# The bias of the attention's exponentials, made on ScalarE column by column instead of on VectorE

## The chip, the cores and the metric

The kernel runs on one core of a Trainium2 chip. The metric is the device time of one execution in microseconds. A core has TensorE (matrix products and transposes, with weight loads beside them), VectorE, ScalarE, GpSimd and SyncE, each with its own in-order queue of instructions; they wait for each other by semaphores. In the profile they are PE, PEld, DVE, ACT, POOL and SP.

## The reference

One layer of a hybrid encoder trunk for 2048 tokens of width 1024. After an RMSNorm a common projection feeds three groups of heads: a state-space layer, differential attention, and a gated linear recurrence (HGRN2). Their outputs go through one output projection and are added to the stream; then follow a second RMSNorm, a gated MLP with a causal convolution, and a last RMSNorm. The part that matters here is the attention, with 6 heads, two softmax maps to a head, and a bias that falls with distance:

```python
def attend(args):
    q_blk, blk = args
    q_pos = blk * Q_BLOCK + jnp.arange(Q_BLOCK)
    sc = jnp.einsum('bqhcd,bkhcd->bhcqk', q_blk, k).astype(jnp.float32) * scale
    dist = jnp.abs(q_pos[:, None] - k_pos[None, :]).astype(jnp.float32)
    visible = (k_pos[None, :] // CHUNK) <= (q_pos[:, None] // CHUNK)
    bias = jnp.where(visible[None], -slopes[:, None, None] * dist[None], MASK_VALUE)
    p = jax.nn.softmax(sc + bias[None, :, None], axis=-1)
    w = p[:, :, 0] - lam * p[:, :, 1]
    return jnp.einsum('bhqk,bkhd->bqhd', w, v)
```

`c` is the map (0 or 1), `h` the head, and a block has 128 queries. The softmax subtracts each row's maximum, so every block needs one number per query and map before its exponentials can run.

## The kernel before

The tokens are cut into 16 blocks of 128 queries. `phase_attn` runs twice, first over the blocks 0 to 7 of all six heads, then, in its lean form with fewer buffers, over the blocks 8 to 15: 96 pairs of head and block. For one of them `scores` does the following. For each map it makes the scores in pieces of up to 512 keys on TensorE (L832, into one of three PSUM tiles `t_ps`). VectorE adds the distance bias to a piece, writes it to the score tile `t_sc` (one for each map) and carries the running maximum in `t_mx`, a tile of 128 x 2 x 4 with a column for each map and piece (L836, with a short instruction after it that writes the maximum). When both maps are done, VectorE makes the bias of the exponentials, `t_nm`, for both maps at once (L843): minus the slope times the last maximum, plus the constant column `t_lk` of each map, which holds scale factors that the second map is joined with. Then ScalarE takes the exponential of each map in place, with that bias as an operand of one number per partition, and sums it up (L848; a load of the function table stands ahead of it where another function's table is in use).

Behind it come, some steps later, `joined` (VectorE: a reciprocal in L860, a factor in L861, and in L867 the second map added to the first with that factor), `parts` (the weights split into two float16 halves, ScalarE's cast in L890 and GpSimd's subtraction in L891, and then transposed by DMAs on SyncE's queue in L898), `values` (the products with V on TensorE, L913) and `put` (ScalarE reads them out of PSUM, L875 and L877).

The attention is not alone. It is one of two streams that `weave` joins, each with costs that say how far it may run ahead of the other: while the attention runs, the other stream does the HGRN2 group (tiles `g_`), an early part of the output projection (`o_`) and then the MLP (`f_`), whose splitting of numbers into float16 halves goes through the helper `split` (ScalarE in L55, VectorE or GpSimd in L61, L63 and L59). L1863 is a helper of the MLP that adds or subtracts on VectorE or GpSimd. The order in which the instructions of one engine finally stand is not the order of the program text: the program is built with a planner that simulates the engines' times and places what is ready,

```python
    with tile.TileContext(nc, schedule_with_timeline_sim=True) as tc:
        tile_trunk_kernel(tc, *args)
```

and it sets the semaphores by what each instruction reads and writes.

Of the kernel before, what the change touches and what calls it, by code (L numbers as in the profile page):

```python
# [13 lines left out]
AF = mybir.ActivationFunctionType  # L14
ALU = mybir.AluOpType
# [17 lines left out]
SLOPES = [2.0 ** (-8.0 * (i + 1) / NH) for i in range(NH)]  # L33
# [720 lines left out]
def phase_attn(K, A, QKd, Vd, Yd, i0, i1, s_bufs, lean):  # L754
# [5 lines left out]
    tc, nc = K.tc, K.nc  # L760
    V = nc.vector
    NT = i1 - i0
    LM = 128 * i1
    base, nlam, lk, gc = A.base, A.nlam, A.lk, A.gc
    with ExitStack() as es:
# [50 lines left out]
        def scores(h, i, sc):  # L816


            H = heads[h]
            n_ = i - i0  # L820
            L = 128 * (i + 1)
            qt = kq[h, i // 4]
            mx = mp.tile([128, 2, 4], F32, tag="mx", name="t_mx")
            nm = mp.tile([128, 2], F32, tag="nm", name="t_nm")
            bs = base[:, S - L:S]
            nchunk = (L + 511) // 512
            sc += [sp.tile([128, LM], F32, tag="s", name="t_sc") for c in range(2)]
            for c in range(2):
                for j in range(nchunk):
                    k0, k1 = 512 * j, min(L, 512 * (j + 1))  # L830
                    ps = ps_s.tile([128, 512], F32, tag="s", name="t_ps")
                    nc.tensor.matmul(  # L832
                        out=ps[:, 0:k1 - k0], lhsT=qt[:, c, 128 * (i % 4):128 * (i % 4) + 128],
                        rhs=H.k[:, c, k0:k1], start=True, stop=True,
                    )
                    V.tensor_tensor_reduce(  # L836
                        out=sc[c][:, k0:k1], in0=ps[:, 0:k1 - k0], in1=bs[:, k0:k1], scale=1.0,
                        scalar=-3e38 if j == 0 else mx[:, c, j - 1:j],
                        op0=ALU.add, op1=ALU.max, accum_out=mx[:, c, j:j + 1],
                    )  # L840
                    if c == 0 or j < nchunk - 1:
                        yield 1
            V.scalar_tensor_tensor(  # L843
                out=nm, in0=mx[:, :, nchunk - 1], scalar=-SLOPES[h], in1=lk,
                op0=ALU.mult, op1=ALU.add,
            )
            for c in range(2):
                nc.scalar.activation(  # L848
                    out=sc[c][:, 0:L], in_=sc[c][:, 0:L], func=AF.Exp, scale=SLOPES[h],
                    bias=nm[:, c:c + 1], accum_out=H.la[:, c, n_:n_ + 1],  # L850
                )
            yield 1
# [127 lines left out]
        for h in range(NH):  # L980
            if lean and h > 0:
                load_k(h)
            if h + 1 < NH and not lean:
                load_k(h + 1)
            heads[h] = Head(h)
            for i in range(i0, i1):
                if i % 4 == 0:
                    kq.pop((h, i // 4 - 1), None)
                    load_q(h, i // 4 + 1)
                if i == i0 + 4 and h + 1 < NH:  # L990
                    for n in range(len(stages)):
                        while queues[n] and queues[n][0][2][0] < h:
                            step(n)
                    load_v(h + 1)
                while len(queues[0]) > s_bufs // 2 - 1:
                    step(0)
                t = (h, i, [])
                n = 2 * (i // 4 + 1)
                for _ in scores(*t):
                    slot += 1  # L1000
                    behind()
                    yield (2 * (i + 1) + 1) / n
                enter(0, t)
            yield 4
# [1130 lines left out]
```

## Time and profile before

| | |
|---|---|
| time, median of 3 runs | 2758.4 us (2749.91 to 2762.81) |
| the profiled execution's own time | 2750.61 us |
| its span, from the first instruction to the last | 2748.9 us |
| granted TensorE clock, mean | 0.928 |
| busy: TensorE, VectorE, ScalarE, GpSimd | 88%, 70%, 46%, 49% of the span |
| first and last bias instruction (L843) | 424.0 and 1914.1 us |

How to read the rows that follow. A row of a group names the line, the engine, the operation, what it writes and reads, its shapes, and how often it ran; behind the first bar stand its busy time in us and the mean of one in ns, behind the second the time in which the engine sat idle just before it, and what ended that. A row of the timeline has the start (us from the span's start), the length, and the instruction. A row of waits has who waited for whom, the total in us, how many times, and the longest. In a row of stretches, the busy time of each engine is followed by its number of instructions.

### The profile page before, as it was taken

To read this page: it belongs to the slowest core of one execution; us is meant where nothing else is said; L and a number is where in the kernel's file an instruction comes from. 1 tells how busy PE (TensorE), PEld (TensorE's weight loads), DVE (VectorE), ACT (ScalarE), POOL (GpSimd) and SP (SyncE) were. 2 spreads that over 40 slices of the span, in tenths; PEclk is the share of its full clock that TensorE was granted. 3 is DMA by queue.
4 is the path that set the end of the run, shared out by engine and by line. 5 is a ranking of instruction groups with operands and counts; after the bars stand their busy time and mean duration, and the time that the engine had idled before them with its cause. 6 is when DMAs were issued, how large, how long until landed. Compare 5 with 4: busy or idle time off the path is not lost. (4 is left out here: it accounts for less than half of the span.)

```text
span 2748.9 us, 42509 instructions
## 1 busy us (share of the span) xinstructions
PE 2429.6 (88%) x15438; PEld 1365.9 (50%) x15438; DVE 1924.5 (70%) x3497; ACT 1255.9 (46%) x2270; POOL 1357.3 (49%) x1149
## 2 busy tenths in 40 slices
PE   5998888988988899759998888599989999999998
PEld 4655547767766665334443334244435444444444
DVE  7567746888888785698678998966464655455565
ACT  6333344666656453465446566533144433333221
POOL 5788602444534442267656866615232444444280
PEclk8999999999988878869999999799999999999999
DMA  7675555565665446655555566598785655554733
GB/s 242 234 222 196 172 159 120 117 139 121 112 142 126 92 116 180 165 132 146 180 174 150 168 165 173 185 285 260 256 285 184 219 158 150 162 157 138 282 97 123
DMA packets 556738, 473.06 MB, mean 172 GB/s; under 512 B 277296, under 2 KB 433264, under 8 KB 555504
## 3 DMA queue, kind: packets, MB, share of 16 engines
q1 hardware_dynamic: 534352, 429.97, 55.1%
q10 hardware_dynamic: 22176, 40.38, 4.0%
q8 instruction: 121, 1.98, 0.3%
q14 instruction: 89, 0.73, 0.1%
HBM read 290.35 MB, written 125.83 MB: 151 GB/s over the span
## 5 line engine op out<-in xcount | busy, mean ns | idle before, releaser
L96 PE MATMUL f_pm<-f_q,f_w 128*128 128x512 f16 x3696 | 839.2, 387 | 34.5 <-DVE f_u L1863 10.4
L96 PEld LDWEIGHTS <-f_w 128*128 128x128 f16 x3696 | 363.6, 99 | 502.7 <-issue 77.0
L1786 PE MATMUL f_pd<-f_dw,f_da 128*128 128x512 f16 x1848 | 411.0, 384 | 8.4 <-DVE f_r L1764 7.0
L891 POOL TENSOR_TENSOR t_sc<-t_sc 128x1024 f16<-128x1024 f32 (+7 forms) x144 | 256.8, 1796 | 274.4 <-ACT t_sc L890 247.1
L1786 PEld LDWEIGHTS <-f_da 128*128 128x128 f16 x1848 | 182.0, 99 | 231.5 <-issue 21.5
L848 ACT ACTIVATE t_sc<-t_sc,t_nm 128x128 f32<-128x128 f32 (+7 forms) x192 | 228.9, 1194 | 81.6 <-DVE t_nm L843 81.0
L832 PE MATMUL t_ps<-t_k,t_q 96*128 96x512 f16 (+2 forms) x480 | 168.9, 386 | 100.6 <-DVE t_mx L836 93.3
L836 DVE CUSTOM_DVE_ANT_0 t_sc<-t_ps,t_base,t_mx 128x512 f32<-128x512 f32 (+3 forms) x288 | 185.2, 644 | 24.7 <-PE t_ps L832 15.5
L61 DVE TENSOR_TENSOR f_a<-f_t,f_a 128x512 f16<-128x512 f32 x132 | 155.6, 1200 | 53.4 <-ACT f_a L55 53.0
L867 DVE SCALAR_TENSOR_TENSOR t_sc<-t_sc,t_a 128x1024 f32<-128x1024 f32 (+7 forms) x144 | 180.5, 1279 | 1.3
L96 PE MATMUL g_pv<-g_w,g_h 128*128 128x256 f16 x1152 | 154.3, 292 | 18.7 <-ACT g_w L55 11.8
L913 PEld LDWEIGHTS <-t_wt 128*128 128x128 f16 x2448 | 108.2, 104 | 110.2 <-DMA t_wt<-t_sc 49.2
L1863 POOL TENSOR_TENSOR f_t<-f_t,f_t 128x512 f32<-128x512 f32 x66 | 100.9, 1543 | 121.2 <-ACT f_a L55 109.8
L96 PE MATMUL g_pq<-g_h,g_w 128*128 128x256 f16 x1152 | 149.7, 288 | 10.4 <-DVE g_sg L1160 5.4
L913 PE MATMUL t_po<-t_v,t_wt 128*128 128x64 f16 x2448 | 121.5, 202 | 38.3 <-DMA t_wt<-t_sc 33.0
L1863 POOL TENSOR_TENSOR f_k<-f_k,f_k 128x512 f32<-128x512 f32 x88 | 124.7, 1417 | 59.3 <-ACT f_k L1895 26.0
L1617 DVE SCALAR_TENSOR_TENSOR f_t<-f_u,f_cw,f_t 128x1024 f32<-128x1024 f32 x88 | 125.5, 1426 | 32.5 <-ACT f_t L1615 31.7
L890 ACT CAST t_sc<-t_sc 128x1024 f16<-128x1024 f32 (+7 forms) x144 | 111.7, 792 | 77.9 <-DVE t_sc L867 73.6
L836 DVE CUSTOM_DVE_ANT_0 t_sc<-t_ps,t_base 128x512 f32<-128x512 f32 (+2 forms) x192 | 121.0, 633 | 34.8 <-PE t_ps L832 21.4
L96 PEld LDWEIGHTS <-g_h 128*128 128x128 f16 x1152 | 118.0, 104 | 50.6 <-issue 22.5
L55 ACT ACTIVATE f_a<-f_t 128x512 f16<-128x512 f32 x154 | 94.8, 627 | 96.4 <-DVE f_a L61 32.1
L55 ACT ACTIVATE f_w<-f_sum 128x512 f16<-128x512 f32 x110 | 69.1, 628 | 150.0 <-DVE f_sum L139 65.1
(335 smaller groups left out, 4490.0 us busy)
## 6 DMA issues: line engine op xcount, KB each, us to landing
f_w<-Wd SPq DMA_DIRECT2D x231, 256.0 KB, 3.0
Wd<-f_w SPq DMA_DIRECT2D x154, 256.0 KB, 2.1
Ad<-f_a ACTq DMA_DIRECT2D x154, 256.0 KB, 2.6
f_da<-Ad SPq DMA_DIRECT2D x42, 768.0 KB, 5.1
g_h<-Hd SPq DMA_DIRECT2D x24, 1024.0 KB, 6.7
f_dst<-in_w_down_dram SPq DMA_DIRECT2D x48, 512.0 KB, 4.6
o_wst<-in_w_out_dram SPq DMA_DIRECT2D x24, 512.0 KB, 5.5
f_wst<-in_w_gate_dram SPq DMA_DIRECT2D x22, 512.0 KB, 5.5
```

What stands on the lines that cost most here:

```text
L55: nc.scalar.activation(out=hi, in_=src, func=AF.Copy, scale=scale)
L61: nc.vector.tensor_tensor(out=lo, in0=src, in1=hi, op=ALU.subtract)
L96: nc.tensor.matmul(out=out, lhsT=lhs(a, k), rhs=rhs(b, k), start=(n == 0), stop=(n == 3 * nk - 1))
L832: nc.tensor.matmul(out=ps[:, 0:k1 - k0], lhsT=qt[:, c, 128 * (i % 4):128 * (i % 4) + 128], rhs=H.k[:, c, k0:k1], start=True, stop=True,)
L836: V.tensor_tensor_reduce(out=sc[c][:, k0:k1], in0=ps[:, 0:k1 - k0], in1=bs[:, k0:k1], scale=1.0, scalar=-3e38 if j == 0 else mx[:, c, j - ...
L848: nc.scalar.activation(out=sc[c][:, 0:L], in_=sc[c][:, 0:L], func=AF.Exp, scale=SLOPES[h], bias=nm[:, c:c + 1], accum_out=H.la[:, c, n_:n_ ...
L867: V.scalar_tensor_tensor(out=sc[0][:, k0:k1], in0=sc[1][:, k0:k1], scalar=a[:, 1:2], in1=sc[0][:, k0:k1], op0=ALU.mult, op1=ALU.add,)
L891: nc.gpsimd.tensor_tensor(out=hl[:, LM + k0:LM + k1], in0=sc[0][:, k0:k1], in1=hl[:, k0:k1], op=ALU.subtract,)
L913: nc.tensor.matmul(out=po, lhsT=wt[:, w, b, :], rhs=vt[:, b, 64 * v:64 * v + 64], start=(b == 0 and w + v == 0), stop=(b == i and w == 1),)
L1617: V.scalar_tensor_tensor(out=t0, in0=u[:, c:n + c], scalar=cw[:, c, m:m + 1], in1=t0, op0=ALU.mult, op1=ALU.add,)
L1786: nc.tensor.matmul(out=ps[t], lhsT=a[:, q, x, tk], rhs=w[:, y, q, :], start=(first and q + x + y == 0), stop=(last and q == n - 1 and y == 1),
L1863: eng.tensor_tensor(out=o, in0=a, in1=b, op=op)
```

## The change

The one VectorE instruction that made both columns of `t_nm` goes. In its place ScalarE makes each column just ahead of the exponential that uses it, with the function Identity, the slope as scale and the column of `t_lk` as bias: two short instructions for each pair of head and block, 192 in all. In the new file they stand in L844 and the exponential stays in L848.

```diff
-            V.scalar_tensor_tensor(
-                out=nm, in0=mx[:, :, nchunk - 1], scalar=-SLOPES[h], in1=lk,
-                op0=ALU.mult, op1=ALU.add,
-            )
             for c in range(2):
+                nc.scalar.activation(
+                    out=nm[:, c:c + 1], in_=mx[:, c, nchunk - 1:nchunk], func=AF.Identity,
+                    scale=-SLOPES[h], bias=lk[:, c:c + 1],
+                )
                 nc.scalar.activation(
                     out=sc[c][:, 0:L], in_=sc[c][:, 0:L], func=AF.Exp, scale=SLOPES[h],
                     bias=nm[:, c:c + 1], accum_out=H.la[:, c, n_:n_ + 1],
```

## The prediction, made before the changed kernel ran

> **What bounds the kernel now.** I read the page first: the busy shares, then the chain.
>
> ```profile
> PE 2429.6 (88%) x15438; PEld 1365.9 (50%) x15438; DVE 1924.5 (70%) x3497; ACT 1255.9 (46%) x2270; POOL 1357.3 (49%) x1149
> PE 27%; DVE 4%; DMA 4%; issue 3%; POOL 2%; ACT 2%; SPq 0%; DVEq 0%; ACTq 0%; POOLq 0%
> ```
>
> TensorE is busy for 88% of the span, but that is an average over stages, and the followed chain reaches only the last part. The edited line runs in the attention, so I read the busy times by stretch next (us of each stretch: PE, PEld, DVE, ACT, POOL, then clock, DMA share, GB/s).
>
> ```profile
> 424.00:700.00 276.00, 245.68 (x2554) 199.12 (x2551) 224.77 (x647) 172.36 (x436) 120.12 (x112) 0.93 0.58 123
> 700.00:1000.00 300.00, 256.23 (x2632) 202.92 (x2632) 246.82 (x602) 166.90 (x321) 139.92 (x113) 0.87 0.54 119
> 1000.00:1300.00 300.00, 246.65 (x1548) 131.01 (x1549) 226.61 (x425) 152.04 (x269) 140.63 (x92) 0.82 0.60 154
> 1300.00:1600.00 300.00, 264.38 (x1425) 121.45 (x1423) 244.85 (x337) 152.05 (x255) 200.47 (x131) 0.96 0.56 166
> 1600.00:1790.00 190.00, 144.61 (x892) 68.01 (x891) 172.08 (x281) 118.03 (x183) 126.70 (x79) 0.88 0.60 174
> 1790.00:1925.00 135.00, 128.65 (x710) 59.44 (x710) 81.94 (x123) 52.32 (x77) 46.36 (x21) 0.95 0.86 272
> ```
>
> From 424 to 1600 us TensorE is idle for 30.3 + 43.8 + 53.4 + 35.6 = 163 of 1176 us, while VectorE is busy for 943 (80%) and ScalarE for 643 (55%). From 1600 to 1790 TensorE falls to 76% and VectorE stands at 91%: there VectorE sets the pace. From 1790 on TensorE is at 95% and nothing that this change touches can matter. The waits from 424 to 1925 us (total, times, longest) say who stands behind whom:
>
> ```profile
> PE t_ps L832 <- DVE t_mx L836: 92.8, 67, 11.6
> ACT t_sc L848 <- DVE t_nm L843: 81.0, 48, 5.8
> DVE t_a L860 <- ACT t_sc L848: 50.4, 49, 3.3
> ```
>
> TensorE's largest wait in this stage is for VectorE's score-and-maximum pass (L836). ScalarE waits for the bias in 48 of 96 blocks, and VectorE in 49 for the exponentials. So VectorE is the first limit after TensorE, and ScalarE is the one with room.
>
> **The change part by part.**
>
> *Removed: 96 VectorE instructions (L843).* The group, its durations (least, median, longest), its sums in two stretches, and one instance beside GpSimd:
>
> ```profile
> L843 DVE SCALAR_TENSOR_TENSOR t_nm<-t_mx,t_lk 128x2 f32<-128x2 f32 x96 | 33.9, 355 | 0.7
> L843 DVE SCALAR_TENSOR_TENSOR t_nm<-t_mx,t_lk x96: 134/156/1650, 424.0 to 1914.1; 128x2 f32<-128x2 f32 x96
> ...
> 424.00:700.00 276.00, 12.53 (x40) 0.93 0.58 123
> 1600.00:1790.00 190.00, 5.77 (x9) 0.88 0.60 174
> ...
> 596.08 1.64 POOL L891 TENSOR_TENSOR t_sc<-t_sc 128x768 f16<-128x768 f32 x1 [1.87 <-ACT t_sc L890]
> 596.10 1.64 DVE L843 SCALAR_TENSOR_TENSOR t_nm<-t_mx,t_lk 128x2 f32<-128x2 f32 x1
> ```
>
> At the median of 156 ns the 96 would be 15.0 us; they take 33.9. The difference of 18.9 us is waiting inside the instruction: at 596.10 it lasts 1.64 us and ends with the GpSimd instruction that began 0.02 us before it. When the line goes, VectorE is relieved of at least 15.0 us (the next instruction inherits every stall) and at most 33.9 (none). I take 30, since what follows mostly reads PSUM for one input, as L836 does.
>
> The Trainium skill has a rule here ("SBUF — State Buffer", Who interferes with whom): a VectorE instruction with two SBUF inputs contends with a GpSimd instruction that reads SBUF and is fully blocked, while ScalarE never waits for another engine. The row at 596.10 agrees with the first half, no row here can show the second for this operation; by the rule all 18.9 us would go, without it they might move to ScalarE with the work.
>
> How much reaches the end? From 1600 to 1790 us, with VectorE at 91%, I count L843 nearly in full: −5 of its 5.77. From 424 to 1600 it holds up to 33.9 − 5.77 = 28.1 us (all but the last few lie there). A microsecond of VectorE there is worth at least what TensorE waited for its maxima per microsecond of VectorE work, 92.8/943 = 0.10, and about TensorE's whole idle time, 163/943 = 0.17: −2.8 to −4.8, I take −3.5, for the 30 that I count. Together −8.5; the ends are −1.4 − 1.4 = −2.8 (156 ns each, 9 of them in full and 87 at 0.10) and −33.9 (all of it on the path).
>
> *Moved: ScalarE need not wait for both maxima.* The old line took both columns, so the first exponential stood behind the last score pass of the second map. Now the first needs only its own column.
>
> ```profile
> L836 DVE CUSTOM_DVE_ANT_0 t_sc<-t_ps,t_base,t_mx 128x512 f32<-128x512 f32 (+3 forms) x288 | 185.2, 644 | 24.7 <-PE t_ps L832 15.5
> ```
>
> That row is cut by the next one in use, so I only take its mean: 644 ns a pass, one to four passes to a block's second map. In the 48 blocks where ScalarE was early it can begin up to 0.64 to 2.6 us sooner; of its 81.0 us of waiting perhaps half goes, and with it half of the 50.4 us that VectorE waits behind L848. At 0.10 to 0.17 for a microsecond, 25 us are −2.5 to −4.3; I take −3. Ends: 0 (the first column's instruction is not placed earlier) and −8.6 (all 50.4 at 0.17).
>
> *Added: 192 ScalarE instructions of 128x1.* No such one is in the trace. Nearest rows: the exponentials by shape, back-to-back instructions, and VectorE's reading of its own fresh result.
>
> ```profile
> L848 ACT ACTIVATE t_sc<-t_sc,t_nm 128x256 f32<-128x256 f32 x12 | 6.0, 499 | 1.7 <-DVE t_nm L843 1.7
> L848 ACT ACTIVATE t_sc<-t_sc,t_nm 128x128 f32<-128x128 f32 x12 | 4.7, 393 | 4.9 <-DVE t_nm L843 4.9
> ...
> 605.20 0.40 ACT L848 ACTIVATE t_sc<-t_sc,t_nm 128x128 f32<-128x128 f32 x1
> 605.49 0.20 ACT L848 ACTIVATION_READ_ACCUMULATOR t_sc<-t_sc,t_nm 128x1 f32 x1
> ...
> 612.28 0.08 DVE L836 DVE_READ_ACCUMULATOR2_ANT t_mx<- 128x1 f32 x1
> 612.39 0.16 DVE L843 SCALAR_TENSOR_TENSOR t_nm<-t_mx,t_lk 128x2 f32<-128x2 f32 x1
> ```
>
> 128 columns cost 499 − 393 = 106 ns, so one column with a bias pointer is about 393 − 106 = 287 ns long. A successor starts 605.20 + 0.40 − 605.49 = 0.11 us before the end, so it holds the engine for about 0.18. The exponential that follows reads what it has just written: if it has to wait for that, the nearest row is VectorE's at 612.39, which began 0.03 us after its producer's end: then 0.32 us. So 192 × 0.18 = 35 to 192 × 0.32 = 61 us, I take 0.25, 48 us. Behind a waiting one on ScalarE's queue stand the exponentials, the casts of L890, the PSUM copies of L875 and the issue of ScalarE's own stores; before, all of these stood behind L848's wait. No DMA, and nothing on SP's or GpSimd's queue, is added or moved. The tile of the maxima is now freed by ScalarE; it has three buffers, and the score tiles of the same block, two or three blocks deep, are freed later still (by L898's transposes), so no score pass waits longer for it: 0, and if that cover were gone, up to one such instruction's 0.32 us a block.
>
> What is that worth? From 1600 to 1790 us I look at the chain, first its shares, then two pieces of it (start, us), and last at L848's busy time in the same stretch:
>
> ```profile
> by line: issue 25.2%; PE f_pm L96 10.8%; DVE t_sc L836 9.4%; ACT t_sc L848 7.3%; DVE f_t L1617 6.7%; DVE t_sc L867 6.5%; DVE f_a L61 6.1%; DVE f_w L63 4.2%; DMA t_wt<-t_sc 3.9%; DVE f_k L1863 2.0%; DMA f_w<-Wd 1.8%; POOL t_sc L891 1.7%; DVE
> ...
> 1673.36 1.23 DVE t_nm L843
> ...
> 1699.99 1.20 DVE t_nm L843
> ...
> 1600.00:1790.00 190.00, 39.75 (x44) 0.88 0.60 174
> ```
>
> L848 is 7.3% of 190 us, 13.9 us: 35% of the 39.75 us that it is busy in this stretch. 35% of 18 × 0.25 is +1.6. L843 stands in the same chain at 1.2 us a time, which is why I counted it nearly in full. From 424 to 1600 the other 168 columns are 42 us. VectorE's wait for ScalarE's exponentials, 50.4 of 643 us of ScalarE work, gives 0.08 of VectorE's time for one of ScalarE, worth 0.17 at most; even five times that 0.013 makes +2.8. I take +2. Together +3.6; ends 0 (all beside other work) and +61.
>
> *Table loads.* L848 is preceded by a load of the function table in 14 places.
>
> ```profile
> L848 ACT ACT_TABLE_LOAD x14 | 18.0, 1283 | 2.9 <-DVE f_a L61 1.9 <-DVE t_nm L843 0.6
> ...
> 1672.76 1.28 ACT L848 ACT_TABLE_LOAD   x1
> 1674.61 1.90 ACT L848 ACTIVATE t_sc<-t_sc,t_nm 128x1920 f32<-128x1920 f32 x1 [0.56 <-DVE t_nm L843]
> ```
>
> At 1672.76 the load runs while the bias is still being made. An Identity in front that waits for the maximum can push the load behind that wait. ScalarE was idle for only 2.9 us before the 14, so it is mostly late anyway: I take +1; ends 0 and +18.0.
>
> *Sum:* −8.5 − 3 + 3.6 + 1 = −6.9. The profiled execution took 2750.61 us (span 2748.9, 1.7 around it), which is 7.8 under the median of 2758.4, and the runs spread over 12.9. So −6.9 is 2743.7 by the profile and 2751.5 by the median; I name 2748, between them.
>
> **The rivals.** A change of 0.5% is 13.8 us, about what can be told from none.
>
> *A larger gain.* The bias leaves the GpSimd-blocked instruction, and 81.0 us of ScalarE's waits and 50.4 of VectorE's shrink together. If a third of L843's 33.9 and a quarter of those 50.4 reach the end, with ScalarE's cost hidden: −11.3 − 12.6 = −24, 2734. For it speaks the chain from 1600 on; against it, that TensorE's idle time from 424 to 1600 is 163 us with many owners.
>
> *Hidden.* VectorE's freed time becomes waiting for something else (scores, transposes), and ScalarE's is hidden too: 2757. For it: TensorE at 88%.
>
> *Slower: ScalarE's pair of short instructions becomes the delay.* Place: maximum, Identity, wait for its own result, exponential, twice a block, and only then L860. Price: 61 us less L843's 15.0 is 46; with a third on the path, +15, about 2772. It decides when VectorE's wait behind L848 grows from 50.4 by more than the 30 us that VectorE is spared. Against it: ScalarE was early in 48 blocks. The Trainium skill speaks for it ("ScalarE: Activation LUTs", Rules for kernel authors): adds and multiplies belong on VectorE, not on ScalarE; by durations 192 × 0.287 = 55 us against 33.9 bear it out, by occupancy (55% against 80%) the trace does not.
>
> *Identity is not in the loaded table:* 192 blocks of change and back, 384 × 1.283 = 493 us, 3250. Against it: copies, casts and squares stand among the 192 exponentials, with 14 loads only.
>
> Beside all of these the planner's order of instructions can shift everywhere after 424 us, either way, which no row prices; it widens the range.
>
> **How the numbers follow.** Forecast 0.42, larger gain 0.20, hidden 0.20, slower 0.16, tables 0.02. The range runs from 2726 (below the larger gain) to 2774 (above the slower case) and leaves out the far ends of the bounds and the tables; the forecast's own range is 2738 to 2760. Faster by over 0.5% (under 2744.6): the larger gain and a third of the forecast, 0.34. Slower by over 0.5% (over 2772): half of that rival, tables and a bad order, 0.14. Within: 0.52.
>
> **What would show it.** L843 gone from VectorE, and its busy time from 424 to 1925 us down by 25 to 34; 192 rows of 128x1 on ScalarE with a mean of 0.25 to 0.30 us; ScalarE's wait for the maxima well under 81.0; VectorE's wait in L860 under 50.4; 14 or so loads in front of L848. Wrong it would be if the wait in L860 grew, if loads came by the dozen, or if other lines that I do not touch moved by more than these terms.

## The result: 1.4% faster, more than forecast

The changed kernel takes 2721.4 us (median of 4 runs, 2718.75 to 2726.4) against 2759.8 before (the median of four runs, with one more than in the table above): a ratio of 0.9862, with a 95% interval of 0.9841 to 0.9883, or 38 us less. The forecast was 2748 with a range down to 2726, so the sign was right and the size was not. The profiled execution took 2723.9 us, 26.7 less than the one shown of before, which was among the quickest of its kernel. The granted clock was higher, too: 0.934 to 0.937 in these four runs, against 0.928 in the profiled one of before (more on that below).

The profile after. First the page's busy times, then the stretches (columns as before), then the waits from 424 to 1925 us (in all three rows, in "X <- Y", X waits for Y).

```profile
PE 2408.0 (88%) x15438; PEld 1354.2 (50%) x15438; DVE 1873.5 (69%) x3401; ACT 1316.9 (48%) x2470; POOL 1350.7 (50%) x1149
```

```profile
424.00:700.00 276.00, 244.06 (x2488) 197.96 (x2486) 211.46 (x609) 183.58 (x499) 121.82 (x111) 0.89 0.57 121
700.00:1000.00 300.00, 263.81 (x2826) 208.91 (x2824) 250.75 (x623) 194.63 (x398) 142.65 (x117) 0.92 0.58 124
1000.00:1300.00 300.00, 246.25 (x1518) 124.66 (x1517) 212.06 (x381) 153.38 (x282) 140.72 (x94) 0.87 0.62 160
1300.00:1600.00 300.00, 267.07 (x1545) 125.77 (x1544) 254.08 (x381) 185.65 (x313) 207.03 (x136) 0.97 0.60 172
1600.00:1790.00 190.00, 146.10 (x840) 67.28 (x839) 162.60 (x258) 121.42 (x194) 117.16 (x70) 0.86 0.69 204
1790.00:1925.00 135.00, 124.44 (x740) 59.37 (x738) 70.57 (x111) 40.46 (x67) 48.16 (x24) 0.96 0.76 242
```

```profile
PE t_ps L832 <- DVE t_mx L836: 80.2, 63, 7.3
ACT t_nm L844 <- DVE t_mx L836: 83.1, 77, 4.0
DVE t_a L860 <- ACT t_sc L848: 34.5, 39, 2.7
```

VectorE has 51 us less to do and ScalarE 61 more. The second wait is the one to notice: ScalarE waits for the maxima as long as before (83.1 against 81.0 us), only in more and shorter pieces. What fell is VectorE's wait behind the exponentials (50.4 to 34.5) and TensorE's for the maxima (92.8 to 80.2).

The new instructions, their durations, the loads ahead of the exponentials, and the largest other change on VectorE (L867, first before, then after):

```profile
L844 ACT ACTIVATE t_nm<-t_mx,t_lk 128x1 f32<-128x1 f32 x192 | 55.0, 292 | 87.4 <-DVE t_mx L836 83.1 <-DVE t_lk L743 2.4 <-DVE t_yo L63 0.8
L844 ACT ACTIVATE t_nm<-t_mx,t_lk x192: 277/294/376, 429.3 to 1888.2; 128x1 f32<-128x1 f32 x192
L848 ACT ACT_TABLE_LOAD x21 | 26.9, 1283 | 3.7 <-DVE f_a L61 1.8 <-DMA t_q<-QKd 1.0 <-DMA Wd<-f_w 0.4
```

```profile
L867 DVE SCALAR_TENSOR_TENSOR t_sc<-t_sc,t_a 128x1024 f32<-128x1024 f32 (+7 forms) x144 | 180.5, 1279 | 1.3
```

```profile
L867 DVE SCALAR_TENSOR_TENSOR t_sc<-t_sc,t_a 128x1024 f32<-128x1024 f32 (+7 forms) x144 | 164.6, 1169 | 1.6
```

The last bias is made at 1888.2 us instead of 1914.1: 25.9 of the 26.8 us of span were won by then, inside the attention. How a block runs now is seen in the timeline. Here is the block of 128x1664 near 960 us, before:

```profile
966.99 0.08 DVE L836 DVE_READ_ACCUMULATOR2_ANT t_mx<- 128x1 f32 x1
966.99 0.16 DVE L843 SCALAR_TENSOR_TENSOR t_nm<-t_mx,t_lk 128x2 f32<-128x2 f32 x1
967.18 1.68 ACT L848 ACTIVATE t_sc<-t_sc,t_nm 128x1664 f32<-128x1664 f32 x1 [3.47 <-DVE t_nm L843]
968.87 1.67 ACT L848 ACTIVATE t_sc<-t_sc,t_nm 128x1664 f32<-128x1664 f32 x1
970.69 0.16 DVE L860 RECIPROCAL t_a<-t_la 128x1 f32<-128x1 f32 x1
```

and after the change:

```profile
950.34 0.28 ACT L844 ACTIVATE t_nm<-t_mx,t_lk 128x1 f32<-128x1 f32 x1
950.65 1.68 ACT L848 ACTIVATE t_sc<-t_sc,t_nm 128x1664 f32<-128x1664 f32 x1
...
956.79 0.08 DVE L836 DVE_READ_ACCUMULATOR2_ANT t_mx<- 128x1 f32 x1
956.91 0.29 ACT L844 ACTIVATE t_nm<-t_mx,t_lk 128x1 f32<-128x1 f32 x1 [2.40 <-DVE t_mx L836]
957.24 1.68 ACT L848 ACTIVATE t_sc<-t_sc,t_nm 128x1664 f32<-128x1664 f32 x1
959.04 0.17 DVE L860 RECIPROCAL t_a<-t_la 128x1 f32<-128x1 f32 x1 [2.17 <-ACT t_sc L848]
```

Before, both exponentials stand back to back behind the last maximum, and L860 starts 3.6 us after it (966.99 + 0.08 to 970.69). Now the first starts 6.6 us ahead of the second, before the second map's last three score passes; only one exponential is left in the tail, and L860 starts 2.2 us after the last maximum.

This block is no exception. In some 80 of the 96 blocks the score passes of different blocks do not mix in VectorE's order, so that the starts in the timeline give the tail of each. There L860 comes on the mean 4.6 us after the last maximum before, and 3.2 us after the change. The first exponential starts ahead of the last maximum in none of 79 such blocks before, and in 68 of 81 after the change.

### The profile page after: what moved, and what is told of

It is laid out like the page before. It is cut to its first block, busy times and chain, and to the rows that moved or that the text cites. A ratio compares the mean times of both kernels' runs of the same rounds, so it can differ in the third digit from the quotient of the medians.

```text
span 2722.1 us, 42584 instructions
## 1 busy us (share of the span) xinstructions
PE 2408.0 (88%) x15438; PEld 1354.2 (50%) x15438; DVE 1873.5 (69%) x3401; ACT 1316.9 (48%) x2470; POOL 1350.7 (50%) x1149
## 4 chain that ended last, share of the span: by engine, by line
PE 22%; DVE 15%; issue 8%; POOL 7%; ACT 7%; DMA 6%; SPq 1%; ACTq 0%; DVEq 0%; POOLq 0%
PE f_pd L1786 10%; PE f_pm L96 7%; POOL f_k L1863 2%; DVE f_a L61 2%; DMA f_dst<-in_w_down_dram 2%; DVE t_sc L836 2%; DVE f_t L1617 2%; PE o_pm L1493 2%; PE o_pe L1411 2%; DVE t_sc L867 1%; DVE f_w L63 1%; POOL f_u L1863 1%; ACT f_t L1615 1%; ACT f_t L1910 1%; ACT t_sc L848 1%
## 5 line engine op out<-in xcount | busy, mean ns | idle before, releaser
L891 POOL TENSOR_TENSOR t_sc<-t_sc 128x1024 f16<-128x1024 f32 (+7 forms) x144 | 250.6, 1753 | 302.3 <-ACT t_sc L890 279.1
L832 PE MATMUL t_ps<-t_k,t_q 96*128 96x512 f16 (+2 forms) x480 | 165.9, 372 | 94.6 <-DVE t_mx L836 80.2
L848 ACT ACTIVATE t_sc<-t_sc,t_nm 128x128 f32<-128x128 f32 (+7 forms) x192 | 230.5, 1201 | 6.6 <-DVE f_a L61 1.1
L913 PEld LDWEIGHTS <-t_wt 128*128 128x128 f16 x2448 | 106.3, 101 | 121.3 <-DMA t_wt<-t_sc 50.4
L867 DVE SCALAR_TENSOR_TENSOR t_sc<-t_sc,t_a 128x1024 f32<-128x1024 f32 (+7 forms) x144 | 164.6, 1169 | 1.6
L96 PE MATMUL g_pq<-g_h,g_w 128*128 128x256 f16 x1152 | 159.2, 299 | 5.1 <-DVE g_sg L1160 2.7
L96 PEld LDWEIGHTS <-g_w 128*128 128x128 f16 x1152 | 121.3, 107 | 36.2 <-issue 6.4
```

The source lines that it names most:

```text
L96: nc.tensor.matmul(out=out, lhsT=lhs(a, k), rhs=rhs(b, k), start=(n == 0), stop=(n == 3 * nk - 1))
L832: nc.tensor.matmul(out=ps[:, 0:k1 - k0], lhsT=qt[:, c, 128 * (i % 4):128 * (i % 4) + 128], rhs=H.k[:, c, k0:k1], start=True, stop=True,)
L848: nc.scalar.activation(out=sc[c][:, 0:L], in_=sc[c][:, 0:L], func=AF.Exp, scale=SLOPES[h], bias=nm[:, c:c + 1], accum_out=H.la[:, c, n_:n_ ...
L867: V.scalar_tensor_tensor(out=sc[0][:, k0:k1], in0=sc[1][:, k0:k1], scalar=a[:, 1:2], in1=sc[0][:, k0:k1], op0=ALU.mult, op1=ALU.add,)
L891: nc.gpsimd.tensor_tensor(out=hl[:, LM + k0:LM + k1], in0=sc[0][:, k0:k1], in1=hl[:, k0:k1], op=ALU.subtract,)
L913: nc.tensor.matmul(out=po, lhsT=wt[:, w, b, :], rhs=vt[:, b, 64 * v:64 * v + 64], start=(b == 0 and w + v == 0), stop=(b == i and w == 1),)
```

## The experiments

Three theories stood at first: VectorE's relief made the gain (1); the earlier start of the first exponential made it (2); the planner's other order of all instructions made it by chance (3). Ratios are to the kernel before, run on the same chip beside each; to put them beside each other I turn them into microseconds of 2759, by which the change is −38.

**One column at a time, still on VectorE.**

```diff
-            V.scalar_tensor_tensor(out=nm, in0=mx[:, :, nchunk - 1], scalar=-SLOPES[h], in1=lk, ...)
             for c in range(2):
+                V.scalar_tensor_tensor(
+                    out=nm[:, c:c + 1], in0=mx[:, c, nchunk - 1:nchunk], scalar=-SLOPES[h],
+                    in1=lk[:, c:c + 1], op0=ALU.mult, op1=ALU.add,
+                )
```

> The bias stays on VectorE but is made one column at a time, each just ahead of its exponential: VectorE gets 96 short instructions more than before (some 15 to 34 us of work), ScalarE none. Theory 1 (VectorE's relief made the gain): slower than before or equal, 2758 to 2775. Theory 2 (the first exponential need no longer wait for the second map): most of the 38 us appear here too, 2722 to 2740. Theory 3 (the gain is the planner's other order, by chance): anything within some 25 us of 2758, with no relation to either.

Measured 2746.2 us, ratio 0.9951 (0.9935 to 0.9968): −14 us, with more work on VectorE. Theory 1 cannot give that; but the gain is smaller than theory 2 had it (2722 to 2740), and it lies in theory 3's range. What the added work on VectorE costs comes out below.

**The change, with the old instruction put back beside it.**

```diff
+            un = mp.tile([128, 2], F32, tag="un", name="t_un")
+            V.scalar_tensor_tensor(out=un, in0=mx[:, :, nchunk - 1], scalar=-SLOPES[h], in1=lk, ...)
             for c in range(2):
                 nc.scalar.activation(out=nm[:, c:c + 1], ...)
```

> The changed kernel, with the old VectorE instruction added back, once a block, into a tile that nothing reads. VectorE has its old work again, ScalarE keeps the new. Theory 1: the gain is lost, 2750 to 2765. Theory 2: most of it stays, 2722 to 2732. Theory 3: anywhere within some 25 us of 2740.

Measured 2730.5 us, ratio 0.9900 (0.9882 to 0.9917): −28. The instruction put back is as long as the old one was:

```profile
L844 DVE SCALAR_TENSOR_TENSOR t_un<-t_mx,t_lk 128x2 f32<-128x2 f32 x96 | 36.0, 378 | 0.7
```

So 36.0 us of VectorE cost about 10 us of the end, 0.28 for one, and 28 of the 38 us stay without the relief.

**Two harmless instructions, meant to move the planner's order.** One ScalarE copy of 128x1 ahead of each attention pass, in the kernel before and in the changed one:

```diff
+        tiny = mp.tile([128, 1], F32, tag="ty", bufs=1, name="t_ty")
+        nc.scalar.copy(tiny, gc)
         load_k(0)
```

> The kernel before, with one ScalarE copy of 128x1 ahead of each of the two attention passes (two instructions, under 0.5 us of work): it only moves the planner's simulated times, and with them the order on every engine. Theories 1 and 2: within 6 us of before. Theory 3: it moves by 10 us or more, either way, though its work is the same.

> The changed kernel with the same two ScalarE copies. Theories 1 and 2: within 6 us of the changed kernel's 2721.4. Theory 3: it moves by 10 us or more, most likely upwards, since the changed kernel would be a lucky draw.

Before with it: 2760.7 us, ratio 1.0005 (0.9991 to 1.0020). After with it: 2717.5 us, ratio 0.9838 (0.9817 to 0.9859). But the copies did not do what they were written for. In the traces all engines run the same instructions in the same order with and without them, but for the copies themselves and four places among TensorE's 15,438. So these two runs say nothing on theory 3. They show how well one and the same order repeats: within 2 us in the one case, and within 4 to 7 in the other (by the medians and by the ratios). What bears on theory 3 are the kernels whose order did change, which follow.

The granted clock could be a cause of its own. In the runs of before it lies at 0.924 to 0.935 and in those of the change at 0.934 to 0.937. At 0.934 and 0.935 the change took 2719 to 2726 us, and the one run of before with 0.935 took 2754.5: 28 to 36 us are left at an equal clock. A straight line through the 13 runs of before on each of three chips gives 0.9 to 1.4 us less for 0.001 more of clock, so I estimate that for the 0.006 between the means, 6 to 9 of the 38 us go with the higher clock. Whether the change brought that clock about is not shown.

**One ScalarE instruction for both columns, ahead of both exponentials.** It uses the first map's constant for both; the constant cancels when the second map is normalised.

```diff
-            for c in range(2):
-                nc.scalar.activation(out=nm[:, c:c + 1], in_=mx[:, c, nchunk - 1:nchunk], ..., bias=lk[:, c:c + 1])
+            nc.scalar.activation(out=nm, in_=mx[:, :, nchunk - 1], func=AF.Identity,
+                                 scale=-SLOPES[h], bias=lk[:, 0:1])
+            for c in range(2):
```

> One ScalarE instruction of 128x2 makes both columns (both with the first map's constant, which cancels when the second map is normalised), ahead of both exponentials. VectorE is relieved as in the change, ScalarE gets half of the added work, but the first exponential again waits for the second map's last maximum. The runs so far give 9 us for VectorE's relief (the changed kernel with and without the old instruction beside it) and 26 to 29 us for the first exponential's earlier start. If that sum holds: 2745 to 2753. If the gain comes from VectorE's relief and from leaving its queue: 2715 to 2730.

Measured 2764.7 us, ratio 1.0022 (1.0006 to 1.0039): +6. VectorE is relieved in full and nothing is won; my sum of the parts, 2745 to 2753, missed as well. Why the relief shows nothing here, though it shows beside the earlier start, stays open. The +6 itself is no more than what two builds of one order differed by.

**One column at a time on VectorE, with one streamed input.**

```diff
             for c in range(2):
+                V.tensor_scalar(
+                    out=nm[:, c:c + 1], in0=mx[:, c, nchunk - 1:nchunk], scalar1=-SLOPES[h],
+                    scalar2=lk[:, c:c + 1], op0=ALU.mult, op1=ALU.add,
+                )
```

> As the kernel with one VectorE instruction per column, but of a form with one streamed input and the constant as a scalar operand. If that form is not held up by GpSimd's instructions, 192 of some 0.15 us are about 29 us, 54 us less than the 83.4 us of the two-input form, and at 0.25 us of the end for one of VectorE's it is 13 us faster than that kernel's 2746: 2733. If it is held up as well: 2740 to 2748. If only ScalarE's doing it counts: no faster than 2746.

Measured 2733.2 us, ratio 0.9900 (0.9873 to 0.9927): −28. The two forms of the same 192 instructions, first with two streamed inputs, then with one:

```profile
L844 DVE SCALAR_TENSOR_TENSOR t_nm<-t_mx,t_lk 128x1 f32<-128x1 f32 x192 | 83.4, 439 | 1.1
```

```profile
L844 DVE TENSOR_SCALAR t_nm<-t_mx,t_lk 128x1 f32<-128x1 f32 x192 | 37.9, 204 | 0.9
```

The second form is not held up (its longest is 216 ns), and the kernel is 14 us faster by 45.5 us of VectorE, 0.31 for one. With 37.9 us it gives VectorE about the load of the old line (33.9) and ScalarE none. VectorE's busy time in all is 19 us less, mostly because L867 is shorter here too, as it also is in two kernels that gained nothing. So the 28 us are the earlier start, with what follows from it.

**The changed kernel without the earlier start.** Each Identity reads the maxima of both maps.

```diff
             for c in range(2):
+                nm = mp.tile([128, 2], F32, tag=f"nm{c}", name="t_nm")
                 nc.scalar.activation(
-                    out=nm[:, c:c + 1], in_=mx[:, c, nchunk - 1:nchunk], func=AF.Identity,
+                    out=nm, in_=mx[:, :, nchunk - 1], func=AF.Identity,
```

> The changed kernel, with the same 192 ScalarE instructions, but each reads the maxima of both maps (128x2) into a tile of its own, of which its exponential uses one column: VectorE relieved, ScalarE's work the same, and the first exponential again behind the second map's last maximum. Theory 2 (the earlier start of the first exponential is the gain): the gain is lost and ScalarE's added work shows, 2755 to 2775. Theory 1 (VectorE's relief, or leaving VectorE's queue): 2721 to 2735.

Measured 2764.3 us, ratio 1.0023 (1.0003 to 1.0044): +6. Its instructions, its block of 128x1664, VectorE's wait behind the exponentials (from 424 to 1950 us) and its L867, from a profiled execution of 2774.5 us, 10 above the median:

```profile
L844 ACT ACTIVATE t_nm<-t_mx,t_lk 128x2 f32<-128x2 f32 x192 | 46.2, 290 | 63.8 <-DVE t_mx L835 61.0 <-DVE t_lk L743 2.4
...
971.89 0.49 ACT L844 ACTIVATE t_nm<-t_mx,t_lk 128x2 f32<-128x2 f32 x2 [0.20 <-DVE t_mx L835]
972.28 1.67 ACT L848 ACTIVATE t_sc<-t_sc,t_nm 128x1664 f32<-128x1664 f32 x1
973.95 1.67 ACT L848 ACTIVATE t_sc<-t_sc,t_nm 128x1664 f32<-128x1664 f32 x1
...
DVE t_a L860 <- ACT t_sc L848: 59.5, 45, 3.9
...
L867 DVE SCALAR_TENSOR_TENSOR t_sc<-t_sc,t_a 128x1024 f32<-128x1024 f32 (+7 forms) x144 | 161.2, 1146 | 1.4
```

Engine and count are as in the changed kernel, with 290 ns each; what differs is the dependence, and that each handles two columns instead of one. The exponentials are back to back again, L860 waits 59.5 us and comes on the mean 4.5 us after the last maximum, and the whole gain is lost: 44 us lie between the two. At a clock of 0.935 this kernel's one run still took 2758.4 us, 32 to 40 more than the change's two.

That settles it for theory 2. It also leaves little to theory 3: the change and seven other kernels with the earlier start, each in an order of its own, took 2717 to 2746 us, and three orders without it (before, and the two that gained nothing) 2757 to 2765. How much another order alone moves the time was not tried.

**What ScalarE's work costs, ahead of and behind the exponential.** First every Identity a second time ahead of itself, then a second one behind the exponential, which reads that exponential's sum:

```diff
+                un = mp.tile([128, 1], F32, tag="un", name="t_un")
+                nc.scalar.activation(out=un, in_=mx[:, c, nchunk - 1:nchunk], func=AF.Identity, ...)
                 nc.scalar.activation(out=nm[:, c:c + 1], ...)
```

```diff
                 nc.scalar.activation(out=sc[c][:, 0:L], ..., func=AF.Exp, ...)
+                un = mp.tile([128, 1], F32, tag="un", name="t_un")
+                nc.scalar.activation(out=un, in_=H.la[:, c, n_:n_ + 1], func=AF.Identity, ...)
```

> The changed kernel, with every Identity run a second time just ahead of itself into a tile that nothing reads: 192 more ScalarE instructions, some 55 us of rows, 35 us of the engine. If ScalarE's added work is nearly free, as its 55% in this stage says: 2721 to 2726. If it is priced like VectorE's (0.25 of it): 2730 to 2735. If each one is a delay on the chain: 2740 or more.

> The changed kernel, with a second Identity of 128x1 behind each exponential, which reads that exponential's sum into a tile that nothing reads: as much ScalarE work as in the kernel with every Identity doubled (2741.3), but behind the exponential instead of ahead of it. If those 20 us were ScalarE's time as such: 2735 to 2745. If they were delay between the maximum and the exponential: 2719 to 2728.

Measured 2741.3 us, ratio 0.9944 (0.9924 to 0.9964), and 2717.3 us, ratio 0.9853 (0.9824 to 0.9881). The added groups are alike:

```profile
L845 ACT ACTIVATE t_un<-t_mx,t_lk 128x1 f32<-128x1 f32 x192 | 55.9, 291 | 114.3 <-DVE t_mx L836 111.2 <-DVE t_lk L743 2.4
```

```profile
L853 ACT ACTIVATE t_un<-t_la,t_lk 128x1 f32<-128x1 f32 x192 | 54.6, 290 | 2.1 <-DVE f_a L61 0.5
```

Ahead of the exponential they cost 23 us against the change, behind it none (−2, within the interval). So ScalarE's time is free here, and delay between a maximum and its exponential is not.

**The pair written earlier in the program**, right behind its own map's score passes.

```diff
+            def bias_exp(c):
+                nc.scalar.activation(out=nm[:, c:c + 1], ..., func=AF.Identity, ...)
+                nc.scalar.activation(out=sc[c][:, 0:L], ..., func=AF.Exp, ...)
...
+                    if j == nchunk - 1:
+                        bias_exp(c)
                     if c == 0 or j < nchunk - 1:
                         yield 1
```

> The changed kernel with each map's pair (Identity and exponential) written right behind that map's own score passes, so that the planner ranks the first pair ahead of the second map's scores. If the first exponential's earlier start is what pays, this gives the same or somewhat more: 2710 to 2722. If the planner already places it as soon as it is ready: 2718 to 2724.

Measured 2718.4 us, ratio 0.9854 (0.9833 to 0.9875), the changed kernel's within its interval. In the traces all engines have the changed kernel's order: the planner wrote the same program out of both texts, and where the pair stands in the text does not matter.

**One column on each engine.** First map on ScalarE and second on VectorE, and the other way round (VectorE in the form with one streamed input):

```diff
+                if c == 0:   # in the other kernel: c == 1
                     nc.scalar.activation(out=nm[:, c:c + 1], ..., func=AF.Identity, ...)
+                else:
+                    V.tensor_scalar(out=nm[:, c:c + 1], in0=mx[:, c, nchunk - 1:nchunk], ...)
```

> The first map's column on ScalarE as in the change, the second map's on VectorE in the form with one streamed input (0.2 us each, 96 of them, 19 us). By 0.25 to 0.29 us of the end for one of VectorE's that costs 5; the second exponential, which ends the block's chain, comes some 0.1 us sooner a block, and ScalarE has 96 instructions less. If delay ahead of the second exponential counts: 2710 to 2722. If only VectorE's time counts: 2724 to 2730.

> The other way round: the first map's column on VectorE, the second's on ScalarE. The same work on each engine as in the kernel with the first on ScalarE. If only the engines' work counts: the same time as that one within 5 us. If the step ahead of the second exponential counts: 5 to 15 us slower than it.

Measured 2731.3 us, ratio 0.9897 (0.9876 to 0.9918), and 2735.2 us, ratio 0.9908 (0.9879 to 0.9937). They are not told apart, and they are 10 and 13 us behind the change. That a second exponential released by VectorE would do better (2710 to 2722) is a miss, and so, by a little, is 2724 to 2730. Some 5 us are VectorE's 19 us of work at 0.28; the rest is open.

## Why the prediction was right or wrong

- *The step that failed is the term for the first exponential's earlier start, taken as −3.* Its mechanism was named; its size was not 3 but 28 us (on VectorE, at about the old load) to 44 (the change against the same instructions without it). I had priced it by what the waits show: half of ScalarE's 81.0 us, and VectorE's 50.4 behind L848 at 0.17 at most, so that even its upper end, −8.6, was no bound. ScalarE's wait did not fall at all. What the earlier start shortened is the tail of the blocks, whether or not somebody was seen to wait there: one exponential of about 1.2 us (median 1194 ns before) less between the last maximum and L860, 96 times, 115 us of delay; the timelines have 1.4 us a block. 28 to 44 us are 0.24 to 0.38 of the 115. Everything behind L860 (L867, the cast, the transposes, the products, and the score tiles that come free) starts earlier by it. Through which of these the time reaches the end was not tried apart, and a part of it goes with the higher clock.
- *VectorE's relief*, −8.5: the size holds beside the earlier start (10 us for 36.0, 0.28 for one, which is also what −8.5 for 30 is). That is luck in part. Without the earlier start the relief shows nothing: both kernels that move the work to ScalarE and keep the old dependence end at +6. And my lower price of 0.10 mixed two stretches: the 92.8 us of waits are from 424 to 1925 us, the 943 us of VectorE from 424 to 1600, where the waits are 54.4 us, so 0.06; in the same way the 50.4 us behind the exponentials are 38.0 there. VectorE's busy time from 424 to 1925 us fell by 36 us, a little more than the 25 to 34, and in the whole kernel by 51, where L867 lost 15.9 as well. The two kernels at +6 have a shorter L867, too (163.6 and 161.2 us), and gained nothing, so I count it as a by-product.
- *ScalarE's added work*, +3.6: the lengths were right (292 ns against 287, and the exponential starts 0.03 us after its Identity's end, 950.34 + 0.28 to 950.65, as VectorE's row had it). But it was priced as ScalarE's time, which is free; as delay ahead of the exponentials a second set costs 23 us. What the first set costs was not tried alone.
- *Table loads*, +1: 21 stand ahead of L848 instead of 14, 9 us of ScalarE's time. What they cost was not tried apart. Identity forced none by itself: no load stands ahead of L844, and the kernel with one VectorE instruction per column, which has no Identity, has 20.
- *The rivals.* "A larger gain", 2734, was the nearest; 0.20 for it was too little, and the range should have reached below it by more than 8 us, as no row priced the shorter tail. "Hidden" and "slower" are near what comes without the earlier start. The planner's order, which widened the range, has no measured size. The forecast of 2748 was not the sum but a point between two bases, 10 us under the median where the sum had 6.9; by either the gain was forecast too small.
- *The two rules of the Trainium skill.* "SBUF — State Buffer", Who interferes with whom: 439 ns a piece with two streamed inputs and 204 with one agree with it, and so does ScalarE, whose longest Identity is 376 ns where VectorE's longest was 1650; all of the stalls went. "ScalarE: Activation LUTs", Rules for kernel authors, that adds and multiplies belong on VectorE: with the dependence unchanged the runs agree (+6 us on ScalarE, about the spread of two builds); what paid was the dependence, not the engine, and then ScalarE was 10 us better than VectorE.

## What to carry to other kernels

Look at what an edit does to the dependences before counting its engine time: an instruction that makes operands for two consumers ties both to the later of its inputs, and splitting it was worth 28 us at an equal load, and 14 where it added 50 us of work to VectorE. Bound the worth of a shorter chain by its length times the number of blocks (here 0.24 to 0.38 of that came out), not by the idle time that the profile shows just ahead of it: a shorter tail can pay also where nobody seems to wait. Where a planner writes the order, build a harmless edit beside the change, and look in the traces whether the order did move: here it had not, and the run showed only how well a time repeats.

## What the runs showed of the hardware

The same bias column took VectorE 439 ns on the mean with the constant as a second streamed input and 204 ns with it as a scalar operand: 45.5 us over 192 instructions of 128x1. In the first form, the 91 that overlapped with a GpSimd instruction took 760 ns on the mean and the other 101 took 149; all 55 of over 400 ns ended together with a GpSimd instruction, to within 40 ns. In the second form those beside GpSimd took 203 ns and the others 204. ScalarE made the column in 292 ns, with a spread of 277 to 376: 292 beside a GpSimd instruction and 291 otherwise.
